# RWKV states and right sides in one unpadded tile per direction, read by products of 64 rows by 64 columns

## The chip, the cores and the metric

The kernel runs on one core of a Trainium2 chip. What counts is the device time of one execution in microseconds; the median of several runs is given. PE is the matmul engine (TensorE), PEld its loading of weights, DVE the vector engine, ACT the scalar engine, POOL is GpSimd, and SP issues most of the DMAs.

## What is computed

The reference is a two-layer backbone of 256 context tokens and 256 latent tokens with 1024 channels, in float32. Layer 0 is a bidirectional Mamba-2 mixer and a SwiGLU; layer 1 is a bidirectional RWKV-7 mixer ("Mixer 2" in the kernel's list of changes) and a mixture of 8 experts, of which each token takes two. Each sublayer is modulated by the conditioning vector and gated.

The RWKV-7 mixer has 16 heads of 64 channels. For each head and direction it runs a recurrence over the tokens, on a state S of 64 x 64: S is multiplied by a decay, corrected along one vector, and a product of key and value is added; the output of a token is the product of its receptance with the state. Context tokens read context alone, latent tokens read both.

## The kernel before

**Tiles and stages.** Heads stand in pairs: a parity `par` of 0 or 1 is the half of the 128 partitions (`ROWS[par]`) that a head takes. Tokens are worked in chunks, and inside a chunk the recurrence becomes a triangular system, whose inverse `Tt` is prepared by `invert` (blocks of 32x32, lines L1164 to L1219). `features` makes keys, decays and gates; what a chunk needs then stands in tiles `C` (padded by zeros, one per parity), `KR` and `BT`. Only the state has to go through the chunks one after the other. That is `scan`, and the change lies in it.

**The scan.** One call works on 8 heads (4 pairs), 4 chunks `i` and 2 directions `d`. Its inner list `HP` has 8 products, 4 pairs by 2 parities. A step has three parts. First the right sides: 8 products of C with Q and 8 of KR with the state Z collect in a bank `px` (tile `xu`), and DVE and ACT copy half each to the tile `xz`. Then 8 products of Tt with xz give the solutions `pu`; beside them the old state goes through an identity into the bank `acc`, and, for the latent tokens (`j`), 8 products of Z with KR go to the output `py`. ACT and DVE copy the solutions to Q. Last, 8 products of BT with Q are added to the bank of the state, DVE multiplies it by the decay `dc` and writes Z, and for latent tokens Q times C joins the output.

**Four scans** run; their DVE copies of the right sides stand at 1129 to 1163, 1280 to 1298, 1401 to 1461 and 1536 to 1582 us. The first is woven with the inversion of the second direction's chunks, the second with the making of features, the third with the stages of the other half of the heads, the last with the normalization of the mixer's output and its output projection. In the output projection's rows L803 to L805 are its three products.

**What sets the order.** The generators yield between parts and `weave` takes them in turn; then the framework's scheduler, which works by simulated times, orders the instructions of each engine at build time. On PE it puts products of several tiles between each other, one by one. Each engine then runs its list in order and waits on semaphores. So an edit that makes a product shorter or longer in the scheduler's model also moves others.

**Names in the rows.** `acc<-Sz,cst` is the identity product, `xu<-Sz,KR` KR by Z into the right sides, `acc<-KR,Sz` Z by KR into the output, `xu<-xz,Tt` the solutions, `xu<-Q,C`, `acc<-Q,BT` and `acc<-C,Q` the products that the edit leaves alone. In the profile a matmul's tile stands as rows*columns of the array (128*64), and a float32 product of 64 columns has two records.

Of the kernel before, what the change touches and what calls it, by code (L numbers as in the profile page):

```python
# [10 lines left out]
F32 = mybir.dt.float32  # L11
# [4 lines left out]
ALU = mybir.AluOpType  # L16
# [121 lines left out]
def tile_backbone(ctx: ExitStack, tc: tile.TileContext, T, out: bass.AP, dbg=None, stop=99):  # L138
    nc = tc.nc
    V, S, G, PE, SY = nc.vector, nc.scalar, nc.gpsimd, nc.tensor, nc.sync  # L140
# [10 lines left out]
    def dump(name, ap):  # L151
        if dbg is not None and name in dbg:
            SY.dma_start(dbg[name], ap)

    def mark(name):
        if dbg is not None and "marks" in dbg:
            dbg["marks"].append((name, nc.get_next_instruction_name()))

    def bank(name, bufs):
        return ps.tile([128, 512], F32, name=name, bufs=bufs)  # L160
# [16 lines left out]
    ident = C["ident"]  # L177
# [188 lines left out]
    with ExitStack() as es:  # L366
# [25 lines left out]
        par = mp.tile([128, 2, 64], F32, name="par")  # L392
# [8 lines left out]
        p = misc()  # L401
# [3 lines left out]
        v, e, q, q2, s, daTM = [part(i) for i in range(6)]  # L405
# [16 lines left out]
        for dst, ws in ((cum, ("tri_f", "tri_b")), (tail, ("tail_f", "tail_b")), (etot, ("ones", "ones"))):  # L422
            p = misc()
# [14 lines left out]
        for d in range(2):  # L438
            p = misc().bitcast(BF16)
# [169 lines left out]
    with ExitStack() as es:  # L609
        op = es.enter_context(tc.tile_pool(name="op", bufs=1, reuse_waits="tile"))  # L610
# [9 lines left out]
        for n in range(4):  # L620
# [4 lines left out]
            for m in range(2):  # L625
                t = op.tile([128, NT], F32, name="ot", bufs=2)
# [64 lines left out]
    rc = rw.enter_context(tc.tile_pool(name="rc", bufs=1, reuse_waits="tile"))  # L691
# [25 lines left out]
    V.tensor_scalar(oka, ka2, -1.0, 1.0, op0=ALU.mult, op1=ALU.add)  # L717
    ROWS = (slice(0, 64), slice(64, 128))


    Sz = [[rc.tile([128, 8, 64], F32, name=f"Sz{d}{par}") for par in range(2)] for d in range(2)]
    xz = [[rc.tile([128, 4, 64], F32, name=f"xz{d}{par}") for par in range(2)] for d in range(2)]
    for t in Sz[0] + Sz[1] + xz[0] + xz[1]:
        G.memset(t, 0.0)

    def weave(*gens):

        live = [list(g) for g in gens]
        while live:
            for it in list(live):  # L730
                for _ in range(it[1]):
                    if len(it) > 2:
                        with tc.high_priority(it[2]):
                            r = next(it[0], it)
                    else:
                        r = next(it[0], it)
                    if r is it:
                        live.remove(it)
                        break
# [77 lines left out]
    def normed(up, j):  # L817

        mj = 1 - j

        U = [up.tile([128, 258], F32, name=f"U{k}") for k in range(DK)]
        xx = [up.tile([128, 256], F32, name=f"xx{k}") for k in range(DK)]
        for k in range(DK):
            G.memset(U[k][:, 0:258:257], 0.0)
            if j:
                S.dma_start(xx[k], xd[:, k, :])
        A = up.tile([128, 8], F32, name="modA")
        V.tensor_scalar(A, mods[1][:, 8:16, mj], 1.0, None, op0=ALU.add)
        V.tensor_mul(A, A, vec[:, VEC["norm1_g1"]:VEC["norm1_g1"] + 8])

        def norm(up, k):
            t = up.tile([128, 256], F32, name="sq", bufs=2)
            V.tensor_mul(t, xx[k] if j else X[:, k, :256], rbl if j else rbx[:, :256])
            S.activation(U[k][:, 1:257], t, AF.Identity, scale=A[:, k:k + 1], bias=mcol(1, 0, k, mj))
        return U, xx, norm
# [391 lines left out]
    def scan(F, un, y=None):  # L1227

        j, k0 = un.j, un.k0
        ks = slice(k0, k0 + 4)  # L1230
        Q = F["Q"]
        HP = [(h, par) for h in range(4) for par in range(2)]
        mm = lambda o, a, b, first=False, end=False: PE.matmul(o, a, b, start=first, stop=end, skip_group_check=True)
        for i in range(4):
            st = []
            for d in range(2):
                c = ORD[d][i]
                C, KR, Z = un.C[d][c], un.KR[d][c], Sz[d]
                bx = bank("xu", 2).rearrange("p (z h v) -> p z h v", z=2, h=4)
                px, pu = bx[:, 0], bx[:, 1]  # L1240
                for h, par in HP:
                    mm(px[ROWS[par], h, :], C[par][:, h, 0:64], Q[par][:, c, k0 + h, :], first=h == 0)
                for h, par in HP:
                    mm(px[ROWS[par], h, :], KR[:, h, 0:64], Z[par][:, k0 + h, :], end=h == 3)
                V.tensor_copy(xz[d][0][ROWS[0]], px[ROWS[0]])
                S.copy(xz[d][1][ROWS[1]], px[ROWS[1]])
                st.append((c, C, KR, un.BT[d][c], Z, pu))
                yield
            ac = []
            for d in range(2):  # L1250
                c, C, KR, BT, Z, pu = st[d]
                ba = bank("acc", 2)
                bv = ba.rearrange("p (z h v) -> p z h v", z=2, h=4)
                pz, py = bv[:, 0], bv[:, 1]
                if not (j and i == 3):
                    for par in range(2):
                        mm(ba[ROWS[par], 0:256], ident[:, ROWS[par]], Z[par][:, ks, :].rearrange("p h v -> p (h v)"), first=True)
                if j:
                    for h, par in HP:
                        mm(py[ROWS[par], h, :], Z[par][:, k0 + h, :], KR[:, h, 64:128], first=i == 3 and h == 0)  # L1260
                for h, par in HP:
                    mm(pu[ROWS[par], h, :], un.Tt[:, d, 4 * c + h, :], xz[d][par][:, h, :], end=h == 3)
                S.copy(Q[0][ROWS[0], c, ks], pu[ROWS[0]])
                V.tensor_copy(Q[1][ROWS[1], c, ks], pu[ROWS[1]])
                ac.append((pz, py))
                yield
            for d in range(2):
                c, C, KR, BT, Z, pu = st[d]
                pz, py = ac[d]
                if not (j and i == 3):  # L1270
                    for h, par in HP:
                        mm(pz[ROWS[par], h, :], BT[:, par, h, :], Q[par][:, c, k0 + h, :], end=h == 3)
                    for par in range(2):
                        V.tensor_tensor(Z[par][ROWS[par], ks], pz[ROWS[par]],
                                        un.dc[d][ROWS[par], :, c:c + 1].to_broadcast([64, 4, 64]), op=ALU.mult)
                if j:
                    for h, par in HP:
                        mm(py[ROWS[par], h, :], Q[par][:, c, k0 + h, :], C[par][:, h, 64:128], end=h == 3)
                    dst = y[:, c, ks, :]
                    if i < 2:  # L1280
                        S.copy(dst, py)
                    else:
                        V.tensor_add(dst, dst, py)
                if i < 2:
                    for par in range(2):
                        G.memset(Q[par][ROWS[par], c, ks], 0.0)
                yield
            un.steps = i + 1
# [92 lines left out]
    if True:  # L1381
        fks = ctx.enter_context(ExitStack())
        fk = fks.enter_context(tc.tile_pool(name="fk", bufs=1, reuse_waits="tile"))
        F.update({n: fk.tile([128, 8, 256], F32, name=n) for n in ("k", "kk", "r")})
        F.update({n: [fk.tile([128, 256], F32, name=f"{n}{d}") for d in range(2)] for n in ("hw", "ha")})
        for t in F["hw"] + F["ha"]:
            G.memset(t, 0.0)
        uxs = ctx.enter_context(ExitStack())
        ux = uxs.enter_context(tc.tile_pool(name="ux", bufs=1, reuse_waits="tile"))
        base = normed(ux, 1)  # L1390

        vx1 = lambda k: (ux.tile([128, 256], F32R, name=f"xx{k}"), ux.tile([128, 258], F32R, name=f"U{k}")[:, :256])
        xv1 = []
        with tc.tile_pool(name="up1", bufs=1, reuse_waits="tile") as up:
            mark("F1S01")
            gf = features(up, F, "kgwar", 9, 2, 5, base, vx=vx1, later_x=xv1, eng=(G, G, G, V))
            next(gf)
            weave((gf, 5), (chain(gi, scan(F0, D1)), 1))
        q0.close()
        for d in range(2):  # L1400
            dump(f"S{d}", Sz[d][0])
        if stop <= 5:
            return

# [18 lines left out]
    with tc.tile_pool(name="tp2", bufs=1, reuse_waits="tile") as tp:  # L1423
        bks = operand_tiles(tp)
        mark("S10A11")
        L1 = Unit(1, 1, r1, L0.Call)
        weave((scan(F, L0, y), 1), *stages(tp, r1, F, L1, 2, bks, SHARED, lambda i: i < L0.steps))
# [170 lines left out]
    if True:  # L1598
# [3 lines left out]
        for k0 in (0, 4):  # L1602
            p = misc()
# [28 lines left out]
        for r in range(2):  # L1632
            v = t1(f"v{r}")
# [6 lines left out]
            h = ti(f"oh{r}")  # L1640
# [9 lines left out]
        p = misc()  # L1650
# [5 lines left out]
        p = misc()  # L1656
# [206 lines left out]
```

## Time and profile before

| | |
|---|---|
| median of 3 runs | 2649.88 us (2646.11 to 2653.32) |
| the profiled execution | 2658.37 us |
| its span | 2656.5 us |
| busy PE, DVE, ACT, POOL | 92%, 77%, 55%, 13% |
| mean granted TensorE clock | 0.931 of full |
| experts | about 1660 us to the end |

The busy shares are averages over stages with different limits, so the rows below show them by stretches. "Busy" of PE counts modelled ends of pipelined matmuls; where the pace matters, it is read from one start to the next, not from durations, since the records overlap.

### The profile page before, as it was taken

The numbers are of one execution on the slowest core, as the hardware profiler recorded it, in microseconds if no ns is written. First come the engines' busy times: TensorE is split into PE (matmuls) and PEld (weight loads), VectorE is DVE, ScalarE is ACT, GpSimd is POOL, SyncE is SP. The second block draws the span as 40 slices with busy tenths as digits, with TensorE's granted clock in tenths as the row PEclk, the third lists the DMA queues.
The fourth block names the chain that finished last, engine by engine and source line by source line (L and its number), as shares of the span: only waits on it lengthen the run. The fifth ranks groups of instructions, "written<-read, shape, count | busy, mean of one in ns | idle before, by whom it ended". The sixth has DMA issues, their size and how long they took to land. (4 is left out here: it accounts for less than half of the span.)

```text
span 2656.5 us, 44879 instructions
## 1 busy us (share of the span) xinstructions
PE 2440.9 (92%) x17770; PEld 1994.8 (75%) x17770; DVE 2039.1 (77%) x3070; ACT 1457.5 (55%) x2322; POOL 341.9 (13%) x434
## 2 busy tenths in 40 slices
PE   7999998999999978679868797999999999999997
PEld 4777776878888767568767686887888788878875
DVE  5787888667554377687676645999999899989997
ACT  4454545333223265435335225877787777778775
POOL 1011102000000254233432211000000000000001
PEclk9999999999999978577888687999999999999999
DMA  7323232336564221022020116899999899989994
GB/s 260 120 88 102 74 104 80 122 121 201 169 203 140 85 94 48 16 68 80 18 73 2 59 39 265 318 359 341 359 370 358 327 363 368 357 320 368 367 340 158
DMA packets 99211, 511.63 MB, mean 193 GB/s; under 512 B 11648, under 2 KB 19072, under 8 KB 55216
## 3 DMA queue, kind: packets, MB, share of 16 engines
q1 hardware_dynamic: 97520, 506.52, 52.8%
q8 instruction: 141, 2.31, 0.4%
q10 hardware_dynamic: 1472, 2.16, 0.3%
q14 instruction: 78, 0.64, 0.1%
HBM read 506.54 MB, written 2.10 MB: 191 GB/s over the span
## 5 line engine op out<-in xcount | busy, mean ns | idle before, releaser
L1720 DVE TENSOR_TENSOR wlo<-wraw,whi 128x1024 fp32r<-128x1024 f32 x662 | 798.4, 1224 | 69.6 <-ACT whi L1719 49.1
L1719 ACT CAST whi<-wraw 128x1024 fp32r<-128x1024 f32 x662 | 694.3, 1051 | 207.1 <-PE gu L214 111.9
L213 PE MATMUL gu<-wlo,xg 128*128 128x512 f32 x896 | 355.3, 397 | 1.5 <-DVE wlo L1720 0.7
L214 PE MATMUL gu<-whi,xg 128*128 128x512 f32 x896 | 349.8, 391 | 0.0
L212 PE MATMUL gu<-whi,xg 128*128 128x512 f32 x896 | 336.4, 392 | 1.1 <-ACT xg L1739 0.9
L206 ACT CAST whi<-wraw 128x1024 fp32r<-128x1024 f32 (+2 forms) x126 | 129.7, 1030 | 218.4 <-PE acc L213 206.2
L207 DVE TENSOR_TENSOR wlo<-wraw,whi 128x1024 fp32r<-128x1024 f32 (+2 forms) x126 | 151.8, 1205 | 110.0 <-ACT whi L206 109.8
L213 PEld LDWEIGHTS gu<-wlo,xg 128*128 128x128 f32 x896 | 168.5, 188 | 42.3 <-DVE wlo L1720 6.1
L212 PEld LDWEIGHTS gu<-whi,xg 128*128 128x128 f32 x896 | 168.4, 188 | 38.1 <-ACT xg L1739 1.6
L214 PEld LDWEIGHTS gu<-whi,xg 128*128 128x128 f32 x896 | 168.7, 188 | 31.5
L213 PE MATMUL y<-wlo,HT 128*128 128x512 f32 x448 | 178.4, 398 | 2.3 <-DVE wlo L1720 2.0
L212 PE MATMUL y<-whi,HT 128*128 128x512 f32 x448 | 176.6, 396 | 3.0 <-DVE xg L1740 3.0
L214 PE MATMUL y<-whi,HT 128*128 128x512 f32 x448 | 176.1, 393 | 0.0
L212 PE MATMUL acc<-h2hi,whi 128*128 128x512 f32 x352 | 137.4, 393 | 3.4 <-ACT h2hi L343 3.4
L1794 POOL TENSOR_TENSOR wraw<-yx,SH 128x512 f32<-128x512 f32 x4 | 7.5, 1875 | 1022.1 <-DVE yx L1790 1022.1
L213 PE MATMUL acc<-h2lo,whi 128*128 128x512 f32 x352 | 137.4, 391 | 0.0
L212 PE MATMUL acc<-hhi,whi 128*128 128x512 f32 (+1 forms) x328 | 135.8, 414 | 0.8 <-ACT whi L206 0.8
L214 PE MATMUL acc<-h2hi,wlo 128*128 128x512 f32 x352 | 134.7, 391 | 0.3 <-DVE wlo L207 0.3
L213 PE MATMUL acc<-hlo,whi 128*128 128x512 f32 (+1 forms) x328 | 134.1, 409 | 0.0
L214 PE MATMUL acc<-hhi,wlo 128*128 128x512 f32 (+1 forms) x328 | 133.6, 408 | 0.0
L305 POOL TENSOR_TENSOR sqa<-sqa,sq 128x512 f32<-128x512 f32 (+1 forms) x35 | 47.5, 1357 | 579.2 <-issue 311.3
L260 DVE SCALAR_TENSOR_TENSOR wraw<-wraw,scb 128x1024 f32<-128x1024 f32 x56 | 68.5, 1223 | 50.2 <-DMA wraw<-in_w_modT_dram 49.4
(565 smaller groups left out, 5358.5 us busy)
## 6 DMA issues: line engine op xcount, KB each, us to landing
wraw<-in_w_mi_dram SPq DMA_DIRECT2D x219, 1024.0 KB, 5.0
wraw<-in_w_mo_dram SPq DMA_DIRECT2D x112, 1024.0 KB, 5.0
wraw<-in_w_modT_dram SPq DMA_DIRECT2D x56, 512.0 KB, 3.9
wraw<-in_w_ffi_dram SPq DMA_DIRECT2D x44, 512.0 KB, 3.6
wraw<-in_w_mod_dram SPq DMA_DIRECT2D x40, 512.0 KB, 5.0
wraw<-in_w_mb_dram SPq DMA_DIRECT2D x40, 512.0 KB, 4.8
wraw<-in_w_mbo_dram SPq DMA_DIRECT2D x16, 512.0 KB, 4.1
wraw<-in_w_ffo_dram SPq DMA_DIRECT2D x16, 512.0 KB, 3.6
```

Source lines behind the costliest of these rows:

```text
L206: S.copy(hi, raw)
L207: eng[q % len(eng)].tensor_sub(lo, raw, hi.bitcast(F32))
L212: PE.matmul(o, whi, xhi, start=start, stop=False)
L213: PE.matmul(o, whi, xlo, start=False, stop=False)
L214: PE.matmul(o, wlo, xhi, start=False, stop=stop)
L260: V.scalar_tensor_tensor(t, w, 0.5, scb[:, j, :], op0=ALU.mult, op1=ALU.mult, accum_out=mods[l][:, n, j:j + 1])
L305: G.tensor_add(self.acc, self.acc, sq)
L1719: S.copy(hi, raw[:, k:k + 2, :])
L1720: V.tensor_sub(lo, raw[:, k:k + 2, :], hi.bitcast(F32))
L1794: G.tensor_mul(xf[:, tt, 512 * n:512 * n + 512], fs, fg[:, 512 * n:512 * n + 512])
```

## The change

The state of a direction was held in two tiles of 128 partitions, one per parity, each zero on the partitions of the other parity, and the right sides in the same way. Products read all 128 partitions, and the zeros made the other half vanish. Now each direction has one tile for the states and one for the right sides, with both parities in their own partitions, and the products read 64 partitions: the operands on both sides are cut to `ROWS[par]`. The identity product and the update of the state cover all 128 partitions in one instruction, and the two copies of the right sides split the pairs (columns) instead of the parities (partitions).

```diff
-    Sz = [[rc.tile([128, 8, 64], F32, name=f"Sz{d}{par}") for par in range(2)] for d in range(2)]
-    xz = [[rc.tile([128, 4, 64], F32, name=f"xz{d}{par}") for par in range(2)] for d in range(2)]
-    for t in Sz[0] + Sz[1] + xz[0] + xz[1]:
+    Sz = [rc.tile([128, 8, 64], F32, name=f"Sz{d}") for d in range(2)]
+    xz = [rc.tile([128, 4, 64], F32, name=f"xz{d}") for d in range(2)]
+    for t in Sz:
         G.memset(t, 0.0)
...
                 for h, par in HP:
-                    mm(px[ROWS[par], h, :], KR[:, h, 0:64], Z[par][:, k0 + h, :], end=h == 3)
-                V.tensor_copy(xz[d][0][ROWS[0]], px[ROWS[0]])
-                S.copy(xz[d][1][ROWS[1]], px[ROWS[1]])
+                    mm(px[ROWS[par], h, :], KR[ROWS[par], h, 0:64], Z[ROWS[par], k0 + h, :], end=h == 3)
+                V.tensor_copy(xz[d][:, 0:2], px[:, 0:2])
+                S.copy(xz[d][:, 2:4], px[:, 2:4])
...
                 if not (j and i == 3):
-                    for par in range(2):
-                        mm(ba[ROWS[par], 0:256], ident[:, ROWS[par]], Z[par][:, ks, :].rearrange("p h v -> p (h v)"), first=True)
+                    mm(ba[:, 0:256], ident, Z[:, ks, :].rearrange("p h v -> p (h v)"), first=True)
                 if j:
                     for h, par in HP:
-                        mm(py[ROWS[par], h, :], Z[par][:, k0 + h, :], KR[:, h, 64:128], first=i == 3 and h == 0)
+                        mm(py[ROWS[par], h, :], Z[ROWS[par], k0 + h, :], KR[ROWS[par], h, 64:128], first=i == 3 and h == 0)
                 for h, par in HP:
-                    mm(pu[ROWS[par], h, :], un.Tt[:, d, 4 * c + h, :], xz[d][par][:, h, :], end=h == 3)
+                    mm(pu[ROWS[par], h, :], un.Tt[ROWS[par], d, 4 * c + h, :], xz[d][ROWS[par], h, :], end=h == 3)
...
-                    for par in range(2):
-                        V.tensor_tensor(Z[par][ROWS[par], ks], pz[ROWS[par]],
-                                        un.dc[d][ROWS[par], :, c:c + 1].to_broadcast([64, 4, 64]), op=ALU.mult)
+                    V.tensor_tensor(Z[:, ks], pz, un.dc[d][:, :, c:c + 1].to_broadcast([128, 4, 64]), op=ALU.mult)
```

The change moves instructions after the first scan has begun. Two places show how.

The first is on PE, in the last step of the last scan. `Sz_7483` and `Sz_7484` are direction 1's two state tiles, `C_12284` and `C_12285` the two parities of C. The kernel before has there:

```order
L1233 MATMUL xu<-Q_12270,C_12284 64x64 x2
L1233 MATMUL acc<-Sz_7483,cst 64x256
L1233 MATMUL xu<-Q_12271,C_12285 64x64
L1233 MATMUL acc<-Sz_7484,cst 64x256
L1233 MATMUL xu<-Q_12271,C_12285 64x64
L1233 MATMUL xu<-Q_12270,C_12284 64x64
L1233 MATMUL acc<-KR_14365,Sz_7483 64x64
L1233 MATMUL xu<-Q_12270,C_12284 64x64
L1233 MATMUL xu<-Q_12271,C_12285 64x64
L1233 MATMUL acc<-KR_14365,Sz_7484 64x64
L1233 MATMUL xu<-Q_12271,C_12285 64x64
```

Of the changed kernel the same place has this order (`Sz_7482` is now direction 1's only state tile, and the lines of the scan stand one lower):

```order
L1232 MATMUL xu<-Q_12228,C_12242 64x64 x2
L1232 MATMUL acc<-Sz_7482,cst 128x256
L1232 MATMUL xu<-Q_12229,C_12243 64x64
L1232 MATMUL acc<-KR_14311,Sz_7482 64x64
L1232 MATMUL xu<-Q_12229,C_12243 64x64
L1232 MATMUL xu<-Q_12228,C_12242 64x64
L1232 MATMUL acc<-KR_14311,Sz_7482 64x64
L1232 MATMUL xu<-Q_12228,C_12242 64x64
L1232 MATMUL xu<-Q_12229,C_12243 64x64
L1232 MATMUL acc<-KR_14311,Sz_7482 64x64
```

The products of C with Q and of Z with KR alternate in both. What changes is their tiles: before, all use 128 rows by 64 columns; after, the rows with `KR,Sz` use 64 rows by 64 columns, those with `Q,C` still 128 by 64, and the identity product 128 by 128.

The second is on DVE, in the first scan, where the inversion's lines L1164 and L1167 (tiles `BK`, `l`) share the engine with the scan. The kernel before has:

```order
L1164 TENSOR_TENSOR BK_10058<-BK_10017,l_10054 128x255
L1164 TENSOR_TENSOR BK_10058<-BK_10017,l_10054 128x15
L1274 TENSOR_TENSOR Sz_7483<-acc,dc_8230 64x256
L1274 TENSOR_TENSOR Sz_7484<-acc,dc_8230 64x256
L1167 TENSOR_TENSOR BK_10017<-BK_10017,BK_10058 128x15x17
L1167 TENSOR_TENSOR BK_10017<-BK_10017,BK_10058 128x15
```

The changed kernel has there:

```order
L1163 TENSOR_TENSOR BK_10048<-BK_10007,l_10044 128x255
L1163 TENSOR_TENSOR BK_10048<-BK_10007,l_10044 128x15
L1166 TENSOR_TENSOR BK_10007<-BK_10007,BK_10048 128x15x17
L1166 TENSOR_TENSOR BK_10007<-BK_10007,BK_10048 128x15
L1271 TENSOR_TENSOR Sz_7482<-acc,dc_8220 128x256
L1163 TENSOR_TENSOR BK_10048<-BK_10007,l_10044 128x256
```

One update of the state stands where two stood, and one pair of the inversion's operations further back.

## Rows read from the trace of the kernel before

**Rows 1.** The page's first part: busy us, share of the span, instructions.

```profile
PE 2440.9 (92%) x17770; PEld 1994.8 (75%) x17770; DVE 2039.1 (77%) x3070; ACT 1457.5 (55%) x2322; POOL 341.9 (13%) x434
```

**Rows 2.** Table of stretches (length; busy by engine; granted clock; DMA).

```profile
core 0: us, PE busy (x) PEld busy (x) DVE busy (x) ACT busy (x) POOL busy (x), PEclk, DMA share, GB/s
1120.00:1150.00 30.00, 19.16 (x357) 16.36 (x352) 27.61 (x93) 5.05 (x14) 2.96 (x13) 0.75 0.12 37
1522.00:1547.00 25.00, 24.77 (x341) 20.04 (x338) 10.24 (x28) 4.89 (x13) 0.00 (x0) 0.50 0.01 2
1547.00:1592.00 45.00, 43.95 (x783) 38.97 (x781) 20.52 (x52) 14.82 (x37) 12.60 (x16) 0.99 0.15 49
1660.00:2650.00 990.00, 972.38 (x4395) 796.14 (x4393) 913.30 (x884) 764.17 (x819) 7.50 (x4) 0.99 0.90 339
```

**Rows 3.** The states' tile Sz (ns min/median/max, first and last start us, forms).

```profile
L1233 PE MATMUL xu<-Sz,KR x512: 219/222/369, 1123.6 to 1581.9; 128*64 128x64 f32 x171
L1233 PE MATMUL acc<-KR,Sz x256: 219/222/368, 1406.6 to 1584.5; 128*64 128x64 f32 x128
...
L1274 DVE TENSOR_TENSOR Sz<-acc,dc x56: 390/422/429, 1135.8 to 1580.2; 64x256 f32<-64x256 f32 x56
L724 POOL MEMSET Sz<- x4: 527/527/529, 911.0 to 912.4; 128x512 f32 x4
```

**Rows 4.** Lines L842, L1496 and L1500, the same columns as rows 3.

```profile
L842 DVE TENSOR_TENSOR kk<-kk,acc x8: 407/421/422, 989.2 to 1010.9; 128x256 f32<-128x256 f32 x8
...
L1496 DVE TENSOR_TENSOR yx<-yx,gt x16: 282/291/293, 1522.3 to 1606.8; 128x128 f32<-128x128 f32 x16
...
L1500 ACT CAST ohi<-yx x16: 292/298/305, 1522.6 to 1607.9; 128x128 fp32r<-128x128 f32 x16
```

**Rows 5.** The right sides' tile xz, the same columns as rows 3.

```profile
L1233 PE MATMUL xu<-xz,Tt x512: 219/222/369, 1130.1 to 1585.1; 128*64 128x64 f32 x171
L1245 DVE COPY xz<-xu x32: 381/417/418, 1129.2 to 1582.1; 64x256 f32<-64x256 f32 x32
L1246 ACT COPY xz<-xu x32: 366/367/370, 1129.7 to 1583.1; 64x256 f32<-64x256 f32 x32
```

**Rows 6.** Timeline of DVE in the first scan (start us, us, instruction, idle before).

```profile
1135.85 0.88 DVE L1274 TENSOR_TENSOR Sz<-acc,dc 64x256 f32<-64x256 f32 x2
1136.75 0.53 DVE L1167 TENSOR_TENSOR BK<-BK,BK 128x247 f32<-128x247 f32 x2
```

**Rows 7.** Timeline of PE in the last scan, one tile shape, upper clock.

```profile
1580.19 0.34 PE L1233 MATMUL acc<-C,Q 128*64 128x64 f32 x4
...
1580.77 0.34 PE L1233 MATMUL xu<-Sz,KR 128*64 128x64 f32 x4
```

**Rows 8.** Timeline of PE in the third scan, two tile shapes, upper clock.

```profile
1431.40 0.69 PE L1233 MATMUL xu<-xz,Tt 128*64 128x64 f32 x16
1431.91 0.40 PE L1233 MATMUL acc<-Q,BT 128*64 128x64 f32 x6
1432.24 0.68 PE L1091 MATMUL ms<-cst,BK 64*64 64x64 f32 x16
1432.85 0.56 PE L1233 MATMUL acc<-Q,BT 128*64 128x64 f32 x10
```

**Rows 9.** Timeline of PE in the last scan, lower clock.

```profile
1523.42 0.47 PE L1233 MATMUL acc<-KR,Sz 128*64 128x64 f32 x2
1523.82 0.31 PE L1216 MATMUL acc<-M,T 32*32 32x32 f32 x2
1524.07 0.47 PE L1233 MATMUL acc<-KR,Sz 128*64 128x64 f32 x2
...
1540.22 1.07 PE L1233 MATMUL xu<-Q,C 128*64 128x64 f32 x16
1541.08 1.12 PE L1233 MATMUL xu<-Sz,KR 128*64 128x64 f32 x16
```

**Rows 10.** Timeline of all engines in the last scan, a wait of PE.

```profile
1575.66 1.15 PE L1233 MATMUL xu<-xz,Tt 128*64 128x64 f32 x32 [0.78 <-ACT xz L1246]
...
1577.40 0.39 PE L1233 MATMUL xu<-Q,C 128*64 128x64 f32 x5 [0.20 <-DVE Q L1264]
```

More of the change, by code (lines that the diff above doesn't have):

```diff
@@ L1400, in tile_backbone @@
         for d in range(2):
-            dump(f"S{d}", Sz[d][0])
+            dump(f"S{d}", Sz[d])
         if stop <= 5:
```

## The prediction

> **What bounds the kernel now.** I read the busy shares first, then a table of stretches, then the tiles that the edit touches, and last the rows of TensorE one by one where the scan is woven into other work. Over the whole span PE is busy 92% and DVE 77% [rows 1], but that is an average. The stretches say more [rows 2]. From 1660 us on, the experts' weights flow and PE is busy 972 of 990 us: nothing of the edit is there, and what the scans gain or lose before it moves the end one for one. In the first scan (1120 to 1150) DVE is busy 27.6 of 30 us and PE only 19.2: DVE sets the pace. In the last scan it is the other way: PE is busy 24.8 of 25 us from 1522 to 1547, at a granted clock of 0.50 (the lower level, 1.2 GHz), and 43.9 of 45 us from 1547 to 1592, at 0.99 (2.4 GHz), while DVE has 10.2 and 20.5 us of work. The scans between stand between these two. So PE time added in the last scan counts in full, and DVE time saved counts mostly in the first.
>
> **What it removes.** Two updates of a half state, 0.422 us each on 64 partitions, become one on 128 [rows 3]. No such instruction with the same operands is in the trace; the nearest, a DVE tensor_tensor of 128x256 that also reads a PSUM tile, takes 0.421 us [rows 4]: duration goes by columns, not by partitions. That is one 0.42 us saved at each of 28 updates (56 pieces now), 11.8 us of DVE. The 32 copies of the right sides on DVE go from 64x256 at 0.417 us [rows 5] to 128x128. The nearest 128x128 operation takes 0.291 us [rows 4]; it reads no PSUM, so the copy may save anything from 0 to 0.13 us, and I take 0.13: 4.2 us. The 32 on ACT go from 0.367 us [rows 5] to the 0.298 us of a 128x128 cast [rows 4]: 2.2 us. All this is 18 us of engine time, if every piece stood on the path. Where PE has no gap it is worth nothing. In the first scan DVE is the pace, and a pair of updates stands between two steps of the inversion there, 1135.85 to 1136.75, so that the inversion waits 0.9 us for it [rows 6]. There are 8 updates and 8 DVE copies in that scan: 8 x 0.42 + 8 x 0.13 = **-4.4 us**, with 0 and -18 as the bounds. The six memsets taken away are two of the states', 0.527 us each, and four of the right sides' with half as many columns. They run on POOL at 911 us [rows 3], some 200 us before the first scan, and POOL is busy only 3 of 30 us even in that [rows 2]: 0. Without that slack they would be worth at most 6 x 0.53 = 3.2 us.
>
> **What it adds.** The products of the states and right sides (256 of KR by Z, 128 of Z by KR, 256 of Tt by xz, two records each [rows 3, 5]) now use 64 rows by 64 columns of the array, while their neighbours C by Q, Q by C and BT by Q keep 128 by 64. Two questions decide: is such a product faster, and what does it cost to change from one tile shape to the other?
>
> The first. A run of 16 records in 128*64 pieces goes at 0.58/5/4 = 0.029 us a record (six pieces, of which the first and last are in [rows 7], five starts apart). A run of 16 in 64*64 takes 0.61 us from its start to the next [rows 8]; if a change of shape stands in it at what the next lines show, 0.46 is left, again 0.029 a record. Parity 0 uses one corner of the array and parity 1 the opposite one, so as many products are in flight as in two column halves. I take no gain.
>
> The second. Around 1432 us the same two shapes meet at the upper clock [rows 8]: 6 records of 128*64 before the 64*64 run take 0.33 us where 6 x 0.029 = 0.17 would do, and the 64*64 run takes 0.61 where 0.46 would do. That is 0.15 us for every change of shape. Among equal shapes, records of two different products alternate at no cost [rows 7]. At the lower clock 128*64 records alternate with 32*32 ones with a period of 0.65 us for two records each (1523.42 to 1524.07), while 16 records of one shape take 0.86 us, 0.054 each [rows 9]; 0.65 - 0.11 for the first pair and 0 to 0.11 for the second leaves 0.22 to 0.27 us for a change. For 64*64 against 128*64 no row stands at the lower clock; the bounds are 0.15 and 0.27, and I take 0.2.
>
> The Trainium skill's "TensorEngine Tiling (Array Packing)", section "Key Properties", says that changing the tiling mode, not merely the tile, drains TensorE. This speaks against the edit, and the 0.15 us above agrees with it.
>
> Then the count. In the instruction order of PE I compared the tile shape of each matmul with that of the one before. From the first scan product to the last, changes of shape go from 237 to 413, 176 more. Of these, 104 are in the last scan (56 to 160), where the scheduler mixes products of both shapes one by one, as the first place printed above shows: 24 up to the first product of the output projection at 1547, 80 after it. 24 x 0.2 + 80 x 0.15 = **+16.8 us**; bounds 24 x 0.15 + 80 x 0.12 = 13 and 24 x 0.27 + 80 x 0.15 = 18.5. The second scan and the third have 41 more, on PE in stages where PE and DVE take turns: 41 x 0.15 = **+6.2 us**, bounds 0 and 41 x 0.27 = 11. The 31 more in the first scan and its tail lie beside DVE, which has 8 us more work than PE there [rows 2]: 0; without that cover 31 x 0.15 = 4.7 us.
>
> The identity product becomes one of 128 columns of weights for two of 64: at most 28 x 0.1 us less, which the change of shape around it, counted above, eats; 0. Moved instructions: the pieces keep their engines and DMA queues, and one weight load goes out about 19 places earlier on SP, far ahead of its use; 0. The copies are split by columns and no longer by partitions: in the new order too, ACT's copy waits for DVE's, so the chain from DVE's copy to ACT's to PE stays. When PE is late in the last scan, the output projection behind it is late next, then the experts' router, then the weights' conversions, which run close behind PE to the end.
>
> **The sum.** +16.8 + 6.2 - 4.4 = **+18.6 us**, on a profiled execution of 2658.4 us (2656.5 of span and 1.9 around it), so 2677.0. That execution lay 8.5 us over the median of the runs, 2649.9, and the runs to come are medians: 2649.9 + 18.6 = **2668 us**.
>
> **The rivals.**
> A. *The gain on DVE wins* (faster). Where a matmul waits for its data anyway, as PE does for 0.78 us before 1575.66 and 0.20 us before 1577.40 [rows 10], a change of shape in the wait costs nothing. If all 18 us of DVE and ACT time stood on the path and the 145 changes cost 0.05 each, the time is 2649.9 - 18 + 7 = 2639. With all of the gain it decides at 18/145 = 0.12 us a change; with my 4.4 at 0.03. Against it: PE's gaps in the last scan sum to 1.3 of 70 us [rows 2], and no row shows a change that cheap. Chance 0.10.
> B. *Little is left.* Half of the changes fall into waits and the others cost 0.15: 72 x 0.15 - 4.4 = +6.4, 2656. For it: the second and third scans have gaps; against it: the last has none. Chance 0.15.
> C. *The clock stays low.* From 1522 to 1547 PE was busy 24.8 of 25 us at a granted clock of 0.50, and from then on it ran at 0.99 [rows 2]. Should the upper level come 15 us later in the new form, work that takes 7.5 us at the upper one fills these 15, and the changes in it cost 0.05 us more each: some 8 to 20 us by how long it lasts, 2668 + 15 = 2683 in the middle. Chance 0.16.
> D. *Smaller tiles are faster.* Were a 64*64 product to take half the 0.058 us, the 192 of the last scan would save 192 x 0.029 = 5.6 us, and the 448 of the other scans up to 13, of which I leave 5 where PE sets the pace: 2668 - 11 = 2657. The 0.029 a record above speaks against it. Chance 0.07.
>
> Of D, the Trainium skill's same page, section "Theoretical Speedup", gives up to twofold for a dimension of 64 or less; the 0.46 us above doesn't show it with two tiles in use.
>
> **How the numbers follow.** My forecast has 0.52 with its own range 2660 to 2678 (13 + 0 - 4.4 = +9 to 18.5 + 11 = +29 are the outer bounds, less likely together). A measurement of this kernel tells some 0.3%, 8 us, from no change, so below 2642 is faster and above 2658 slower. Faster: A, 0.10. Same: 0.12 of B and 0.04 of D, 0.16. Slower: the rest, 0.74. The range leaves out A and the upper half of C: 2647 to 2686.
>
> **What would show it.** DVE Z updates of 128x256 near 0.42 us, 28 of them, and xz copies near 0.29 us: then the gain was sized rightly. In the last scan, records that alternate 128*64 and 64*64 with gaps of 0.15 us (upper clock) and a stretch from its first product to its last that is some 17 us longer, with PE's idle time as small as now: then the forecast's main term is right. If alternating rows come at 0.03 us apart, changes between these two shapes cost nothing and the forecast is wrong; if the first scan doesn't get shorter, DVE was not its pace. The stretch from 1660 to the end should be as long as before.

## The result, and the profile after

The changed kernel takes 2674.76 us (median of 4 runs, 2669.39 to 2682.97) against 2647.99 for the kernel before (4 runs): ratio 1.0105, 95% interval 1.0077 to 1.0132, 27 us slower. The forecast was 2668 with a range of 2647 to 2686. The profiled execution has a span of 2681.1 us, 24.6 more than before. One of the ten executions of e4 below took 8025 us; its ratio leaves that one out.

The page's first part of the changed kernel, answering to [rows 1]:

```profile
PE 2476.1 (92%) x17714; PEld 2015.7 (75%) x17714; DVE 2022.9 (75%) x3042; ACT 1456.0 (54%) x2322; POOL 335.9 (13%) x428
```

DVE has 16.2 us less to do, as many as 28 updates of 0.42 and 32 copies of 0.13 are, and PE is busy 35 us longer with 56 records fewer. Where that is, the table of stretches shows. The stretches answer to those of [rows 2], with the same columns: the first scan; the last scan up to the first product of the output projection (1552.7), and from there to the last product of Q with the identity (1615.8); and the last 14.5 us of that once more by themselves.

```profile
1116.00:1146.00 30.00, 20.38 (x359) 17.00 (x354) 25.14 (x89) 4.54 (x14) 2.95 (x13) 0.76 0.12 37
...
1519.90:1552.70 32.80, 32.80 (x403) 25.31 (x403) 10.49 (x30) 5.46 (x16) 0.61 (x2) 0.54 0.01 2
1552.70:1615.80 63.10, 62.35 (x711) 50.54 (x711) 16.11 (x42) 12.51 (x33) 12.01 (x14) 0.85 0.11 35
1601.30:1615.80 14.50, 14.50 (x138) 11.16 (x136) 2.41 (x6) 2.49 (x7) 0.00 (x0) 0.50 0.01 2
```

The last scan, from its product of M with C (`xu<-M,C`, just before the state's identity product) to the last of Q with the identity, is this stretch in the kernel before (one row of the same view):

```profile
1520.90:1589.40 68.50, 67.29 (x1125) 57.88 (x1124) 30.34 (x78) 19.27 (x48) 13.01 (x17) 0.80 0.10 33
```

It grew from 68.5 to 95.9 us, by 27.4, and PE is busy 95.2 of the 95.9. DVE, with 26.6 us of work, isn't in question. The rest of the program adds nothing net between these two executions: the last scan began 1 us earlier than before, and from its end to the end of the program it is 1065.3 us for 1067.1.

The tiles of states and right sides came out as the forecast had them (ns min/median/max, as in [rows 3, 5]):

```profile
L1232 PE MATMUL xu<-xz,Tt x512: 216/218/366, 1125.6 to 1607.0; 64*64 64x64 f32 x171
L1244 DVE COPY xz<-xu x32: 259/291/293, 1125.0 to 1601.8; 128x128 f32<-128x128 f32 x32
L1245 ACT COPY xz<-xu x32: 243/266/271, 1125.3 to 1602.2; 128x128 f32<-128x128 f32 x32
...
L1271 DVE TENSOR_TENSOR Sz<-acc,dc x28: 409/425/425, 1131.8 to 1593.2; 128x256 f32<-128x256 f32 x28
```

The update takes 0.425 us, the copies 0.291 and 0.266. A matmul record's median duration hardly changed (218 ns for 222 in Tt by xz): what got longer is mostly not in the records, but between their starts. The timeline of PE in the changed kernel's last scan shows it, first at the lower clock and then at the upper:

```profile
1545.29 0.47 PE L1232 MATMUL xu<-Sz,KR 64*64 64x64 f32 x2
1545.69 0.47 PE L1232 MATMUL acc<-C,Q 128*64 128x64 f32 x2
1546.10 0.47 PE L1232 MATMUL xu<-Sz,KR 64*64 64x64 f32 x2
...
1593.17 0.33 PE L1232 MATMUL xu<-Sz,KR 64*64 64x64 f32 x2
1593.42 0.33 PE L1232 MATMUL acc<-C,Q 128*64 128x64 f32 x2
1593.68 0.32 PE L1232 MATMUL xu<-Sz,KR 64*64 64x64 f32 x2
```

Read the starts, not the durations. One product (two records) of one shape between products of the other comes every 0.26 us (1593.17 to 1593.68, two steps) at the upper clock and every 0.40 at the lower (1545.29 to 1546.10, two steps). In runs of one shape it is 0.06 and 0.11 [rows 7, 9]. So a change of shape costs 0.20 and 0.30 us here, where the sum had 0.15 and 0.20.

### The profile page after: what moved, and what is told of

The parts are those of the page before. It is cut to its first block, busy times and chain, and to the rows that moved or that the text cites. A ratio compares the mean times of both kernels' runs of the same rounds, so it can differ in the third digit from the quotient of the medians.

```text
span 2681.1 us, 44723 instructions
## 1 busy us (share of the span) xinstructions
PE 2476.1 (92%) x17714; PEld 2015.7 (75%) x17714; DVE 2022.9 (75%) x3042; ACT 1456.0 (54%) x2322; POOL 335.9 (13%) x428
## 5 line engine op out<-in xcount | busy, mean ns | idle before, releaser
L1716 DVE TENSOR_TENSOR wlo<-wraw,whi 128x1024 fp32r<-128x1024 f32 x662 | 798.4, 1225 | 68.1 <-ACT whi L1715 47.2
L780 POOL TENSOR_TENSOR wlo<-wraw,whi 128x512 fp32r<-128x512 f32 (+1 forms) x69 | 85.3, 1244 | 184.9 <-ACT whi L779 161.5
```

The lines of the kernel that those rows point to most:

```text
L780: self.eng[self.n % len(self.eng)].tensor_sub(lo, raw, hi.bitcast(F32))
L1716: V.tensor_sub(lo, raw[:, k:k + 2, :], hi.bitcast(F32))
```

## The experiments

Two theories stood after the result. **S**: the loss is the 176 more changes of shape on PE, 104 of them in the last scan. **M**: it is the merged tiles, whose one update and shared tile make more work wait for each other; its variant **Q**: the smaller products are slow in themselves. All runs are on one chip type with the kernel before beside them (medians of 2646.3 to 2648.0 us in the four groups of runs). Changes of shape are counted in PE's instruction order; the stretch of the last scan is taken as above.

| kernel | changes, last scan / all | median us | ratio (95% interval) | last scan us, granted clock |
|---|---|---|---|---|
| before | 56 / 237 | 2648.0 | | 68.5, 0.80 |
| the change | 160 / 413 | 2674.8 | 1.0105 (1.0077 to 1.0132) | 95.9, 0.75 |
| e1 padded tiles, reads cut | 144 / 396 | 2678.3 | 1.0105 (1.0085 to 1.0125) | 88.9, 0.78 |
| e2 the same, last scan alone | 144 / 325 | 2670.6 | 1.0088 (1.0060 to 1.0117) | 89.5, 0.78 |
| e3 one shape, half products | 72 / 259 | 2646.8 | 0.9998 (0.9984 to 1.0011) | 66.1, 0.87 |
| e4 the change, in runs | 65 / 311 | 2648.4 | 0.9991 (0.9977 to 1.0006) | 65.3, 0.85 |
| e5 before, same priority | 45 / 231 | 2641.0 | 0.9983 (0.9969 to 0.9996) | 61.4, 0.85 |
| e6 runs, identity cut | 65 / 281 | 2648.1 | 1.0006 (0.9993 to 1.0019) | 65.2, 0.90 |
| e7 right sides alone | 66 / 274 | 2659.2 | 1.0043 (1.0026 to 1.0060) | 68.1, 0.89 |
| e8 identity cut alone | 145 / 383 | 2669.2 | 1.0085 (1.0059 to 1.0111) | 95.6, 0.75 |
| e9 less DVE and ACT | 60 / 244 | 2634.3 | 0.9949 (0.9930 to 0.9967) | 64.9, 0.89 |
| e10 padded tiles, in runs | 72 / 312 | 2656.0 | 1.0036 (1.0020 to 1.0052) | 67.4, 0.89 |

The profiled execution of a kernel may lie 10 us off its median, so the medians carry the verdicts and the last column says where. The ratios and their intervals are not quotients of the medians and may differ from them by 3 us or so.

**e1: the reads cut, the tiles kept.** The kernel before with nothing but

```diff
+  R = ROWS
...
-  mm(px[ROWS[par], h, :], KR[:, h, 0:64], Z[par][:, k0 + h, :], end=h == 3)
+  mm(px[ROWS[par], h, :], KR[R[par], h, 0:64], Z[par][R[par], k0 + h, :], end=h == 3)
```

and the same cut in Z by KR and Tt by xz.

> Theory S (changes of tile shape): the padded tiles, their paired updates and copies stay as in the kernel before, only the reads of states and right sides are cut to 64 rows. The last scan then has 144 changes of shape (56 before, 160 in the change). In the changed kernel's trace a pair of records of one shape between pairs of the other takes 0.26 us at the upper clock and 0.40 at the lower, against 0.06 and 0.11 in a run of one shape: 0.2 to 0.3 us a change. 88 more in the last scan: +18 to +26 us, about 2670. Theory M (merged tiles): the loss comes from the states and right sides being one tile, whose one update waits for both parities and whose copies wait for each other; then this kernel, which keeps two, is within 6 us of the one before, about 2650.

Measured 2678.3, 30 us over the kernel before. The whole loss is there without a merged tile: M falls, and the reads alone do it. In its profiled execution the last scan grew by 20.4 us, within the 18 to 26 expected. The time is more than that; the other scans have 71 more changes too, which the next run leaves out.

**e2: the same in the last scan alone.** The line for `R` becomes

```diff
+        R = ROWS if j and k0 == 4 else (slice(0, 128), slice(0, 128))
```

> As the run with all reads cut, but cut only in the last scan; the first three scans read all 128 rows as before. Theory S with PE as the pace only in the last scan: nearly the whole loss stands here too, 2666 to 2672 us, within 4 us of the run with all reads cut. If the changes of shape in the other three scans (about 70) cost 0.2 us each on the path, this run is some 10 us or more below that one. Theory M: about 2650.

2670.6: three quarters of the loss. The two medians are 7.7 us apart, and their intervals overlap. They differ by 71 changes of shape, 36 of them in the first scan, so the 7.7 is no test of the 6.2 us that the forecast had for 41 changes in the second and third.

**e3: one shape for all.** The changed kernel with

```diff
-  mm(pz[ROWS[par], h, :], BT[:, par, h, :], Q[par][:, c, k0 + h, :], end=h == 3)
+  mm(pz[ROWS[par], h, :], BT[ROWS[par], par, h, :], Q[par][ROWS[par], c, k0 + h, :], end=h == 3)
```

and the same in C by Q and Q by C.

> The changed kernel with the products of C by Q, BT by Q and Q by C cut to 64 rows as well, so that all but the identity have one shape; this leaves out the other half of each of these sums. Number and width of the products and the order's rules stay. Changes of shape in the last scan fall from 160 to 72, in all from 413 to 259. Theory S: 88 x 0.2 to 0.3 less in the last scan, so about 2652 (2645 to 2660). Theory Q (a product of 64 rows by 64 columns is itself slower than one of 128 rows, whatever stands beside it): still more of them, so 2675 or above.

2646.8. More small products, and the loss is gone: Q falls. The last scan takes 66.1 us.

**e4: the same products in runs.** The changed kernel, with its products of 64 rows put under a higher priority:

```diff
-  for h, par in HP:
-      mm(px[ROWS[par], h, :], KR[ROWS[par], h, 0:64], Z[ROWS[par], k0 + h, :], end=h == 3)
+  with tc.high_priority(400):
+      for h, par in HP:
+          mm(px[ROWS[par], h, :], KR[ROWS[par], h, 0:64], Z[ROWS[par], k0 + h, :], end=h == 3)
```

and likewise around the identity, Z by KR and Tt by xz, with Tt by xz put first.

> The changed kernel with the same instructions, but the products of 64 rows have a higher priority in the scheduler (400 places), so that they come in runs: changes of shape in the last scan fall from 160 to 65, in all from 413 to 311. Theory S: 95 x 0.2 to 0.25 us less, about 2653 (2647 to 2660). Theory Q or M: nothing changes, since tiles, products and copies are those of the changed kernel: 2670 to 2680.

2648.4, 26 us less than the change by the order and the priority alone. The timeline of PE in its last scan, at the upper clock, shows the runs:

```profile
1559.30 0.68 PE L1232 MATMUL acc<-KR,Sz 64*64 64x64 f32 x16
1559.91 0.92 PE L1232 MATMUL xu<-Q,C 128*64 128x64 f32 x24
1560.76 0.68 PE L1232 MATMUL xu<-Sz,KR 64*64 64x64 f32 x16
1561.37 0.33 PE L1232 MATMUL xu<-Q,C 128*64 128x64 f32 x2
1561.63 0.68 PE L1232 MATMUL xu<-Sz,KR 64*64 64x64 f32 x16
```

Sixteen records of 64*64 take 0.61 us from their start to the next (1559.30 to 1559.91), as the other tiles of this shape did before [rows 8]: 16 x 0.029 and 0.15. The short run of two records at 1561.37 takes 0.26 as in the changed kernel. So the forecast's 0.15 is right for long runs and too small for a lone product. What a lone product loses beyond it is its overlap: in a run the products of the two parities go beside each other, and a lone one has none beside it. Rows of the changed kernel show it, where two products of C by Q, one of each parity, stand between lone products of Z by KR:

```profile
1584.69 0.34 PE L1232 MATMUL xu<-Q,C 128*64 128x64 f32 x4
1584.96 0.32 PE L1232 MATMUL acc<-KR,Sz 64*64 64x64 f32 x2
1585.21 0.34 PE L1232 MATMUL xu<-Q,C 128*64 128x64 f32 x4
```

The four records of two products take 0.27 us from start to start, the two of one product 0.25: beside the run rate (0.12 and 0.06) that is 0.15 and about 0.20.

**e5: the control.** The kernel before with the same priority on the same products.

> Control for the run with the products in runs: the kernel before, its padded tiles and 128-row reads, with the same priority (400 places) on the same three groups of products. Changes of shape in the last scan fall only from 56 to 45, in all from 237 to 231. Theory S: 11 x 0.2 to 0.3 us less at most, so 2644 to 2650, no difference to the kernel before that can be told. Theory P (the priority itself shortens the scans, whatever the tiles): it falls by as much as the changed kernel did with it, some 25 us, to about 2623.

2641.0, ratio 0.9983: about 5 us less (the interval reaches from 1 to 8), and not 26. The priority does little where there are few changes of shape to avoid, and up to some 5 of e4's 26 us may be its own. This is also the fastest kernel here that computes everything, the only version found that beats both, by little.

**e6: runs and a small identity.**

```diff
-  mm(ba[:, 0:256], ident, Z[:, ks, :].rearrange("p h v -> p (h v)"), first=True)
+  for par in range(2):
+      mm(ba[ROWS[par], 0:256], ident[ROWS[par], ROWS[par]], Z[ROWS[par], ks, :].rearrange("p h v -> p (h v)"), first=True)
```

in e4, with the priority at 3000.

> The changed kernel with the priority at 3000 places and the identity product cut into two of 64 rows by 64 columns: changes of shape 65 in the last scan, 291 in all, against 65 and 311 of the run with the products in runs (2648.4 us). Theory S: 20 changes fewer, mostly before the last scan, 0 to 4 us less: 2644 to 2649. A version that beats both kernels would have to show here; if the updates and copies saved on DVE and ACT (18 us of engine time) came onto the path once the changes of shape are gone, it would be 2635 or below.

2648.1: nothing more to gain there, and no version better than e5. (Its trace has 281 changes, not the 291 that were expected.)

**e8: the small identity alone**, the same edit in the changed kernel.

> The changed kernel with its identity product (128 by 128) cut into two of 64 by 64, which has the shape of its neighbours. Changes of shape 145 in the last scan (160), 383 in all (413). Theory S: 15 x 0.2 to 0.3 and up to 15 x 0.15 less, 3 to 7 us: about 2670. If the whole loss came from the identity product's 128-column weights between small tiles, 2650.

2669.2, 5.5 us below the change, as 30 changes fewer would give (the intervals overlap, so this alone shows no more than that the identity isn't the cause).

**e7: the right sides alone.**

```diff
-  mm(pu[ROWS[par], h, :], un.Tt[:, d, 4 * c + h, :], xz[d][par][:, h, :], end=h == 3)
+  mm(pu[ROWS[par], h, :], un.Tt[ROWS[par], d, 4 * c + h, :], xz[d][ROWS[par], h, :], end=h == 3)
```

with the copies split by columns, in the kernel before.

> Only the right sides go into one tile: their copies are split by columns (0.29 and 0.27 us for 0.42 and 0.37), and Tt by xz reads 64 rows; the states stay in two padded tiles. Changes of shape 66 in the last scan (56 before), 274 in all (237 before). Theory S: 10 x 0.25 in the last scan and up to 27 x 0.15 in the others, less some 2 us of shorter copies: +1 to +5, 2649 to 2653.

A miss: 2659.2, +11 us by the ratio for 37 more changes, where +1 to +5 was expected. At 0.2 to 0.3 us each they make 7 to 11, but in the profiled execution the last scan is no longer than before. It is the third scan (1397.5 to 1483.6) that takes 86.1 us for 76.6, at a granted clock of 0.81 for 0.91. By the two levels that is 33 us at the lower one for 14; at half the rate the 19 more are worth some 9 us, which is the difference. A lower clock belongs to this kernel and not only to that execution: over the whole span the ten executions have 0.922 to 0.931, mean 0.926, the 29 of the kernel before beside them 0.929 to 0.937, mean 0.933. Whether it is the third scan in all ten, and why, the runs don't show.

**e9: what the saved work is worth.** The kernel before with

```diff
-  for par in range(2):
-      V.tensor_tensor(Z[par][ROWS[par], ks], pz[ROWS[par]],
-                      un.dc[d][ROWS[par], :, c:c + 1].to_broadcast([64, 4, 64]), op=ALU.mult)
+  V.tensor_tensor(Z[0][ROWS[0], ks], pz[ROWS[0]],
+                  un.dc[d][ROWS[0], :, c:c + 1].to_broadcast([64, 4, 64]), op=ALU.mult)
```

and the copies to xz cut to 2 of 4 pairs.

> What the saved DVE and ACT work is worth by itself: the kernel before, all reads of 128 rows, with as much DVE and ACT time taken away as the change takes. The updates of parity 1's states and the copies of half of the right sides' columns are left out, so 28 updates of 0.42 us go and 32 copies on each of DVE and ACT get shorter, while every matrix product stays. Changes of shape 244 (237 before). The sum on record has -4.4 us for it, mostly in the first scan: 2642. If PE hides it all: 2646, no difference; if it all stood on the path, -18: 2628.

2634.3, 13 us less, the interval reaching from 9 to 19. The rows of its two tiles show that what went is what the change takes away (28 updates, copies of 0.28 and 0.26 us):

```profile
L1273 DVE TENSOR_TENSOR Sz<-acc,dc x28: 406/416/418, 1131.0 to 1560.9; 64x256 f32<-64x256 f32 x28
...
L1245 DVE COPY xz<-xu x32: 249/282/283, 1124.2 to 1563.3; 64x128 f32<-64x128 f32 x32
L1246 ACT COPY xz<-xu x32: 260/260/261, 1124.6 to 1563.7; 64x128 f32<-64x128 f32 x32
```

It is rather an upper bound of the gain, since parity 1's products no longer wait for any update at all. Its last scan also had a higher clock (0.89 for 0.80), which may be a part of the 13.

**e10: padded tiles in runs**, e5 with e1's reads: the partner of e4 at the same number of changes.

> The padded tiles of the kernel before with all reads cut to 64 rows and the priority of the run with the products in runs (2648.4 us): changes of shape 312 in all and 72 in the last scan, against 311 and 65 there. What differs between the two is the merged update, the copies by columns and the merged identity product. Theory S with the sum on record: 4.4 us for the updates and copies and 7 x 0.25 for the changes, so about 2654. If updates and copies are worth nothing on the path: 2648 to 2650; if all of them, 2666.

2656.0. Against e4 the merged tiles, with their merged identity product, are 7.6 us faster by the medians and 12 by the ratios, at almost the same number of changes (311 and 312, with 7 more here in the last scan). The change itself against e1 gives less: 3.5 us by the medians and nothing by the ratios, with 17 changes more, so some 3 to 7 us with these at 0.2 each. The gain of the merged tiles lies somewhere from 3 to 13 us; these runs don't tell it better.

## Why the prediction was right, step by step

**The bound.** Right. PE sets the pace of the last scan: PE is busy 27.9 us longer there and the stretch is 27.4 us longer, and no other stage matters as much (e2).

**The duration of the pieces.** Right: 0.425 us for the update (0.42), 0.291 for DVE's copy (0.291), 0.266 for ACT's (0.298). A small product is neither faster nor slower in a run (0.029 us a record in e4); rival D gets nothing.

**The price of a change of shape.** The mechanism is right and the size was off. The term "24 x 0.2 + 80 x 0.15 = +16.8" was taken from runs of 6 and 16 records, while the scheduler puts single products between single products. At 0.30 and 0.20 the same count gives 24 x 0.30 + 80 x 0.20 = 23.2, of the 27.4 measured. Before the output projection the stretch grew from 25.8 (1520.9 to 1546.7) to 32.8, by 7.0 for the 7.2 of this sum; after it from 42.7 to 63.1, by 20.4 for 16. Not every one of these changes stands at a lone product, and a part of the time is the clock's, so the agreement of the sum is in part luck.

**The clock.** Rival C is there in part, in another form than it had. The upper level came 9 us later than before (1556.9 for 1547.9), 7 of them the longer work ahead of it, and at 1601.3 the clock fell again, after 8 us of mostly alternating products (1593.17 on). The last 14.5 us of the stretch ran at 0.50 with PE busy throughout (the row 1601.30:1615.80); before, [rows 2] has 0.99 there. With two levels, 0.5 and 1, the time at the lower one in the last scan is 2 x 0.20 x 68.5 = 27 us before and 2 x 0.25 x 95.9 = 48 after. It goes with the changes of shape: in the last 30 us of the last scan the granted clock is 1.00 in the kernel before and in all seven kernels with 72 changes or fewer there, and 0.76, 0.89, 0.89 and 0.77 in the change, e1, e2 and e8, which have 144 or more. As an estimate, at 0.029 for 0.054 us a record the work of those 14.5 us would take some 8 at the upper level, so the fall is worth up to 7 of the 27.4 us; with the 23.2 of the changes that is more than was measured. Some of the changes stand at a pair of products of both parities, which pays 0.15 and not 0.20; how much of the 27.4 us is the clock's beside the changes was not separated.

**The other scans.** "41 x 0.15 = +6.2 us" was not tested. Between the end of the first scan and the start of the last, the kernel before takes 359.7 us and e2, with the same order up to there, 351.5: one execution differs from the next by more than the term.

**The gain on DVE and ACT.** This step failed in size and in place: "8 x 0.42 + 8 x 0.13 = -4.4 us" was to come from the first scan, and the forecast had said that DVE was not its pace if that scan doesn't get shorter. It did not. From the first product of C by Q to the last it takes 38.1 us before and 39.4 after:

```profile
L1233 PE MATMUL xu<-Q,C x160: 219/222/368, 1123.1 to 1161.2; 128*64 128x64 f32 x160
L1232 PE MATMUL xu<-Q,C x160: 222/222/314, 1118.8 to 1158.2; 128*64 128x64 f32 x160
```

Two terms are in that. With the cut reads and none of the gain (e1) the same stretch takes 41.3 us, with the saved work alone (e9) 36.5; e2, unchanged there, takes 37.9. So the saved work gave about 2 us, not 4.4, though DVE had less to do (25.1 of 30 us busy for 27.6), and the changes of shape, which the forecast hid behind DVE at 0 ("without that cover 31 x 0.15 = 4.7 us"), cost about 3. Over the whole kernel the gain is 3 to 13 us; where the rest of it is, the runs don't show. That the total came out within the range is partly luck: the loss from the changes was put too small and the gain too small as well. 26.8 us measured plus 3 to 13 of gain is 30 to 40 us for 176 changes, 0.17 to 0.23 each, the clock's part included.

**The rivals.** A's opposite sign stayed out, as a change was dearer than its deciding price of 0.12. B didn't come: in the last scan the changes are not hidden in waits (PE is busy 95.2 of 95.9 us).

## What to carry to other kernels

Before cutting products to fewer rows, look at what stands between them: in PE's order, count the places where the tile's shape differs from the neighbour's, and price each by the starts of records in a trace, for runs and for lone products apart. If the shapes must mix, keep each in runs; the scheduler here alternated them one by one, and another order of the same products was worth 26 us. And what an engine off the bound saves is better measured, by taking its work away in the kernel before (e9), than read from busy shares.

## What was unexpected of the hardware

A lone product of 64x64 between two of 128x64 takes 0.26 us from start to start, against 0.06 in a run, at the upper clock (0.40 against 0.11 at the lower): more than four times as long, though its records last 0.22 to 0.27 us, as those of a run do. Two products of opposite parity side by side take hardly longer than one (0.27 for 0.25).

The order of products also goes with the clock that is granted. The change and e4 have the same products to the last one, and in the same stretch 0.75 and 0.85; after 8 us of mostly alternating shapes at the upper level the clock fell to the lower one (1601.3) with PE busy all the time.
